# Decay and rate of an RWKV-7 mixer from three fp32r products each, in a hybrid decoder block

## Chip, cores and metric

One Trainium2 chip, one core of it. The metric is the device time of one execution in microseconds; the time before is 3533.41 us, the median of three runs (3525.39 to 3535.11).

## What is computed

One decoder block on 2048 tokens of width 1024, in float32. Half of the mixer's channels go through chunkwise retention, the other half through an RWKV-7 recurrence over 8 heads of 64 channels; then come a cross-attention into 256 memory tokens, a squared-ReLU MLP of width 4096 and a final norm. The change concerns two vectors of the recurrence, the decay and the rate `a`, which are made from low-rank factors (64 wide each):

```python
r, k, v, w_lr, a_lr, g_lr = jnp.split(p, [...], axis=-1)
w_log = -jax.nn.softplus(-(w0 + jnp.tanh(w_lr) @ w_up)) - 0.5
decay = jnp.exp(-jnp.exp(w_log))
a = jax.nn.sigmoid(a0 + a_lr @ a_up)
...
kk = kk / jnp.maximum(jnp.sqrt(jnp.sum(jnp.square(kk), axis=-1, keepdims=True)), 1e-12)
k = k * (1.0 + (a - 1.0) * k_a)
...
y = wkv7_scan(rh, decay.reshape(B, S, H, d), kh, vh, -kk, kk * ah)
```

## The kernel before

The kernel has two stages. The first (to about 1570 us in the profile) makes the projections, the retention, the recurrence and the products of the memory; the second (the output projection, the attention and the MLP) is not edited.

**Precision.** Large products take each operand as a sum of two fp32r parts, a rounded `hi` and a remainder `lo`, and add three products, hi·hi, hi·lo and lo·hi (`chain3_`). `split` (L181) makes the parts: ScalarE copies (L183), VectorE or GpSimd subtracts (L184). Small products are done in f32 with one call; the profile shows two records for such a call (two passes).

**Tiling of the first stage.** Four blocks of 512 tokens; in a block four pairs of heads, so 16 groups, numbered n = 4·block + pair. The names carry both: `mm13r` is the projection r of block 1, pair 3. The recurrence of a group runs over 8 chunks of 64 tokens.

**The functions around the change.** `lora_wa(b)` projects a block's 512 tokens on the two low-rank inputs, 128 rows in all (rows 0 to 63 of the decay, 64 to 127 of the rate): 24 fp32r products into `mmwa`, the token shift on ScalarE (L388) and VectorE (L389), then tanh on the rows of the decay (L794). The result `wa` has two buffers. `rwkv_prep(n, ...)` prepares a group. It loads the 128x128 factor `wua` (L405), makes the decay's argument `pz` from rows 0 to 63 and the rate's `pa` from rows 64 to 127 by one f32 product each, 128x512 in size, and takes tanh of both (`th` L410, `ta` L414). From `th` VectorE makes the running sums `cum` (L416, L419), ScalarE the exponentials; `sq`, its sums `pss`, the matrices `Mx` and the rest follow. `rwkv_chain` is the recurrence proper: three dependent products (`ch`) for each chunk, with small VectorE and ScalarE operations between them (`rh` L609, `X` L619, L620 and L630).

**What sets the order.** `weave` takes all of this as eight streams and records their instructions by a clock of its own, to which each product adds an assumed time (`mm`: N/2400 us for fp32r, four times that for a long f32 product). The TensorE order that results is kept as it is (`keep_in_program_order`); the other engines' queues are ordered by the scheduler's simulation. The stream `dense` issues the projections, taking for each block the first item of a list that is ready ("A" is `lora_wa`, "K" the keys, "R" the rest of a pair, "Q" the retention). `preps` starts a group once its keys and its block's `wa` are there.

Two pools matter: `ps_sc` has two PSUM buffers, used in turn, one each for `pz` and `pa`; `tp` has one SBUF buffer for a tag, so that all tiles with tag F use the same place one after the other: the retention's rotary part `rbq` (L719, read by GpSimd at L727), `b1` of the preparation, and others.

Of the kernel before, what the change touches and what calls it, by code (L numbers as in the profile page):

```python
# [8 lines left out]
F32 = mybir.dt.float32  # L9
F32R = mybir.dt.float32r  # L10
# [8 lines left out]
P = 128  # L19
# [17 lines left out]
BLK = 512  # L37
# [88 lines left out]
def hybrid_block(tc, a, out, dbg=None, halves=2, stages="012"):  # L126
    nc = tc.nc
    V, A, G, TE, SY, AQ = nc.vector, nc.scalar, nc.gpsimd, nc.tensor, nc.sync, nc.scalar
# [3 lines left out]
    def pinned(ins, us):  # L132

        if te["pin"]:
            tc.keep_in_program_order(ins)
            te["us"] += us

    def mm(o, l, r, start, stop):
        n = int(np.prod(r.shape[1:])) / 2400
        us = n if r.dtype != F32 else 4 * n if n > 0.05 else 0.03 if n < 0.02 else 0.084  # L140
        pinned(TE.matmul(o, l, r, start=start, stop=stop), us)  # L141
# [39 lines left out]
    def split(hi, lo, x, eng):  # L181

        A.activation(out=hi, in_=x, func=AF.Copy)  # L183
        eng.tensor_tensor(out=lo, in0=x, in1=hi.bitcast(F32), op=ALU.subtract)  # L184
# [96 lines left out]
    if "1" in stages:  # L281
        with ExitStack() as ctx:
            e = ctx.enter_context
            act = e(tc.tile_pool(name="act1", bufs=1))
            one = e(tc.tile_pool(name="one1", bufs=1))
            rp = e(tc.tile_pool(name="r1", bufs=1))
            tp = e(tc.tile_pool(name="t1", bufs=1))
            pp = e(tc.tile_pool(name="p1", bufs=1))
            gp = e(tc.tile_pool(name="g1", bufs=2))
            ps_mm = e(tc.tile_pool(name="mm1", bufs=2, space=PSUM))  # L290
            ps_sc = e(tc.tile_pool(name="sc1", bufs=2, space=PSUM))
# [90 lines left out]
            hs = [slice(0, 64), slice(64, 128)]  # L382
# [10 lines left out]
            def proj_cm(w, nm):  # L393
                ps = ps_mm.tile([P, BLK], F32, tag="mm", name=f"mm{nm}")
                yield from chain3_(ps, [((w[0][:, k, :], w[1][:, k, :]), (hT[0][:, :, k, :], hT[1][:, :, k, :])) for k in range(8)])
                return ps

            def rwkv_prep(n, pr, tok0, kS, wa, nm):
# [4 lines left out]
                g4 = [slice(0, 4), slice(4, 8)]  # L403
                lo_ = pp.tile([P, P], F32, tag="wua", name=f"wua{nm}", bufs=1)
                SY.dma_start(out=lo_, in_=a["lora"][pr][:, :P])  # L405

                pz = ps_sc.tile([P, BLK], F32, tag="sc", name=f"pz{nm}")
                mm(pz, lo_[0:64, :], wa[0:64, :], True, True)
                th = tp.tile([P, BLK], F32, tag="A", name=f"th{nm}")
                A.activation(out=th, in_=pz, func=AF.Tanh, scale=0.5, bias=w0h[:, pr : pr + 1])  # L410
                pa = ps_sc.tile([P, BLK], F32, tag="sc", name=f"pa{nm}")
                mm(pa, lo_[64:128, :], wa[64:128, :], True, True)
                ta = tp.tile([P, BLK], F32, tag="B", name=f"ta{nm}")
                A.activation(out=ta, in_=pa, func=AF.Tanh, scale=0.5, bias=a0h[:, pr : pr + 1])  # L414
                yield 0
# [50 lines left out]
                for q in range(8):  # L466
                    b = q % 4
# [319 lines left out]
                AQ.dma_start(out=yscr[tok0 // BLK][p * P : (p + 1) * P], in_=yo)  # L787

            def lora_wa(b):
                wa = one.tile([P, BLK], F32, tag="wa", name=f"wa{b}", bufs=2)  # L790
                w = W.load(a["w_rw"][12], (8, P), "w12")
                ps = yield from proj_cm(w, f"wa{b}")
                shifted(ps, 12, wa, f"wa{b}")
                A.activation(out=wa[0:64], in_=wa[0:64], func=AF.Tanh)  # L794
                return wa

            def lora_g(b):

# [39 lines left out]
            done = {("pg", -1): True, ("pg", -2): True, ("C", -1, 4): True, ("C", -1, NCH): True, ("C", -2, NCH): True, ("Y", -1): True, ("T", -1): True}  # L838
# [53 lines left out]
            def dense():  # L892

                for b in range(nb):
                    early = None
                    if b == 0:
                        early = yield from ret_proj(4, b, None, "v00")
                    yield lambda: ("X", b) in done
                    rt_ = rotary(b)
                    vs = {}  # L900

                    def ready(pr, what):
                        n = 4 * b + pr
                        if what == "A":
                            return n < 5 or ("P", n - 5) in done
                        if what == "K":
                            return ("P", n - 2) in done
                        if what == "R":
                            return ("P", n - 2) in done and (n < 4 or ("O", n - 4) in done)
                        if what == "Q" and pr == 3 and len(plan) > 1:  # L910
                            return False
                        if what == "Q":
                            return ("H", n - 2) in done
                        if what == "G":
                            return ("O", n - 1) in done
                        return True

                    plan = list(PLAN)
                    while plan:
                        yield lambda: any(ready(*i) for i in plan[:AHEAD])  # L920
                        item = next(i for i in plan if ready(*i))
                        plan.remove(item)
                        pr, what = item
                        n = 4 * b + pr
                        nm = f"{b}{pr}"
                        if what == "A":
                            done["wa", b] = yield from lora_wa(b)
                        elif what == "K":
                            done["K", n], = yield from rkv(b, pr, (1,))
                        elif what == "R":  # L930
                            done["R", n] = yield from rkv(b, pr, (0, 2))
                        elif what == "Q":
                            if pr % 2 == 0:
                                v, early = early, None
                                if v is None:
                                    v = yield from ret_proj(4 + pr // 2, b, rt_, f"v{nm}")
                                vs[pr] = vs[pr + 1] = v
                            sg = yield from ret_gate(b, pr)
                            qk = yield from ret_proj(pr, b, rt_, f"q{nm}", pr == 3)
                            done["Q", n] = qk, vs[pr], sg  # L940
                        elif what == "G":
                            done["G", b] = yield from lora_g(b)
                        elif what == "L" and b + 1 < nb:
                            xs.update({(b + 1, t): scaled_x(b + 1, t) for t in range(4)})
                        elif what == "L" and "0" in stages:
                            xs.update({("mem", t): scaled_memory(t) for t in range(2)})
                if "0" in stages:
                    W.alt, W.spare = True, (one, "gmix")
                    yield from memory()
                    W.spare = None  # L950
# [79 lines left out]
    if "2" in stages:  # L1030
        with ExitStack() as ctx:
# [4 lines left out]
            tp = e(tc.tile_pool(name="t2", bufs=2))  # L1036
# [376 lines left out]
```

## Time and profile before

| | |
|---|---|
| median of the runs | 3533.41 us |
| profiled execution | 3526.81 us, span 3525.0 us |
| TensorE busy | 3348.3 us, 95% of the span |
| VectorE, GpSimd, ScalarE busy | 2082.1, 1623.5, 1215.9 us |
| mean granted TensorE clock | 0.973 of 2.4 GHz |

Busy time counts a matmul from its start to its modelled end, and matmuls overlap; what one of them costs is read from the distance of starts in the timeline. A row of the timeline has the start, the duration, engine, line, operation, out<-in, the array rows and columns used where it is a matmul (64*128 is half of the rows), and in brackets the idle time ahead with its releaser.

### The profile page before, as it was taken

What the parts mean: (1) busy time and instruction counts of PE and PEld (TensorE: products, weight loads), DVE (VectorE), ACT (ScalarE), POOL (GpSimd) and SP (SyncE); (2) the same over time, 40 slices, a digit from 0 to 9 for tenths busy, and PEclk for the clock granted to TensorE, in tenths of its full rate; (3) what the DMA queues carried; (4) which work ended last, traced back from release to release, by engine and by line L of the source; (5) the groups of instructions that cost most, each with busy time, mean ns of one, the idle gap of its engine ahead of it and who ended that gap; (6) DMA issues with size and microseconds to landing.
All of it is one profiled execution on the core that took longest, in us unless ns stands there. A gap on an engine that the chain in (4) does not pass through costs nothing.

```text
span 3525.0 us, 57474 instructions
## 1 busy us (share of the span) xinstructions
PE 3348.3 (95%) x23296; PEld 2739.9 (78%) x23296; DVE 2082.1 (59%) x3637; ACT 1215.9 (34%) x1954; POOL 1623.5 (46%) x1325
## 2 busy tenths in 40 slices
PE   7889999999999899989999999999999999999998
PEld 6668777777777777878887888888788878888886
DVE  5765565456555644543866556555748665656557
ACT  4432323232323231334334333333433343333333
POOL 5444323232323232434546555555645465455555
PEclk9999999999999899999999999999999999999999
DMA  7434323332333233383111111111341111111111
GB/s 262 151 130 150 134 93 118 106 130 97 118 112 118 97 98 107 105 305 118 49 37 48 54 48 54 54 49 57 128 161 47 38 48 51 52 54 54 49 54 48
DMA packets 147160, 333.35 MB, mean 95 GB/s; under 512 B 52048, under 2 KB 62800, under 8 KB 146896
## 3 DMA queue, kind: packets, MB, share of 16 engines
q1 hardware_dynamic: 129632, 299.43, 25.5%
q10 hardware_dynamic: 17264, 30.26, 2.4%
q8 instruction: 183, 3.00, 0.3%
q14 instruction: 81, 0.66, 0.1%
HBM read 269.34 MB, written 60.29 MB: 94 GB/s over the span
## 4 chain that ended last, share of the span: by engine, by line
PE 49%; DVE 5%; POOL 2%; issue 1%; ACT 1%; DMA 0%; DVEq 0%; ACTq 0%; POOLq 0%
PE up L141 20%; PE o L141 4%; PE tms L141 4%; PE m3d L141 3%; PE m6d L141 3%; PE m1d L141 2%; PE m5d L141 2%; PE m4d L141 2%; PE m2d L141 2%; PE m7d L141 2%; DVE xr L1140 1%; DVE pe L1252 1%; PE pskv L141 1%; PE m3v L141 1%; PE psqk L141 1%
## 5 line engine op out<-in xcount | busy, mean ns | idle before, releaser
L141 PE MATMUL up<-uc,whi 128*128 128x512 f32 x2048 | 633.0, 390 | 4.8 <-ACT uc L1111 4.8
L141 PEld LDWEIGHTS up<-uc,whi 128*128 128x128 f32 x2048 | 384.6, 188 | 85.9 <-ACT uc L1111 5.7
L141 PE MATMUL up<-uc,wlo 128*128 128x512 f32 x1024 | 398.7, 390 | 0.0
L184 POOL TENSOR_TENSOR wlo<-wraw,whi 128x1024 fp32r<-128x1024 f32 x103 | 254.4, 2470 | 282.1 <-ACT whi L183 271.2
L183 ACT ACTIVATE whi<-wraw 128x1024 fp32r<-128x1024 f32 x175 | 184.8, 1058 | 398.7 <-PE up L141 139.7
L611 POOL TENSOR_SCALAR Sd<-X,PC 64x64 f32<-64x64 f32 x256 | 127.0, 496 | 351.5 <-DVE X L630 335.0
L184 DVE TENSOR_TENSOR wlo<-wraw,whi 128x1024 fp32r<-128x1024 f32 x72 | 104.6, 1454 | 256.5 <-ACT whi L183 256.4
L184 POOL TENSOR_TENSOR wlo<-s,whi 128x1024 fp32r<-128x1024 f32 x60 | 159.3, 2656 | 182.2 <-ACT whi L183 182.2
L141 PEld LDWEIGHTS up<-uc,wlo 128*128 128x128 f32 x1024 | 192.3, 188 | 40.1
L141 PE MATMUL tms<-whi,ub 128*128 128x256 f32 x1024 | 192.2, 286 | 0.0
L184 POOL TENSOR_TENSOR wlo<-bd,whi 128x1024 fp32r<-128x1024 f32 x64 | 165.9, 2594 | 52.3 <-ACT whi L183 52.2
L184 POOL TENSOR_TENSOR f<-au,f 128x1024 fp32r<-128x1024 f32 x40 | 112.1, 2801 | 133.6 <-ACT f L183 133.6
L141 PE MATMUL o<-whi,f 128*128 128x512 f32 x512 | 162.8, 398 | 1.5 <-issue 1.5
L141 PEld LDWEIGHTS tms<-whi,ub 128*128 128x128 f32 x1024 | 161.1, 191 | 0.4
L141 PE MATMUL rmq<-whi,hh 128*128 128x256 f32 x512 | 151.6, 296 | 0.0
L141 PE MATMUL rmq<-whi,hl 128*128 128x256 f32 x512 | 151.2, 295 | 0.0
L141 PE MATMUL rmq<-wlo,hh 128*128 128x256 f32 x512 | 150.9, 295 | 0.0
L1299 ACT ACTIVATE au<-up 128x512 f32<-128x512 f32 x128 | 75.1, 587 | 204.9 <-PE up L141 204.9
L141 PE MATMUL tms<-wlo,ub 128*128 128x256 f32 x512 | 145.4, 284 | 0.0
L619 ACT ACTIVATE X<-ch,rn 64x64 f32<-64x64 f32 x128 | 39.1, 306 | 303.6 <-PE Y L141 269.7
L1071 POOL TENSOR_TENSOR s<-bd,bd 128x1024 f32<-128x1024 f32 x48 | 122.2, 2548 | 30.1 <-DMA bd<-w_down 21.8
L183 ACT ACTIVATE whi<-bd 128x1024 fp32r<-128x1024 f32 x64 | 67.7, 1057 | 189.3 <-PE m2d L141 63.6
(1061 smaller groups left out, 9177.8 us busy)
## 6 DMA issues: line engine op xcount, KB each, us to landing
bd<-w_down SPq DMA_DIRECT2D x64, 512.0 KB
wraw<-w_up SPq DMA_DIRECT2D x64, 512.0 KB
whi<-kepthiw SPq DMA_DIRECT2D x45, 512.0 KB
wlo<-keptlow SPq DMA_DIRECT2D x45, 512.0 KB
whi<-kepthim SPq DMA_DIRECT2D x36, 512.0 KB
wlo<-keptlom SPq DMA_DIRECT2D x36, 512.0 KB
wraw<-w_out SPq DMA_DIRECT2D x32, 512.0 KB
xs<-x SPq DMA_DIRECT2D x16, 512.0 KB
```

The lines of the kernel that those rows point to most:

```text
L141: pinned(TE.matmul(o, l, r, start=start, stop=stop), us)
L183: A.activation(out=hi, in_=x, func=AF.Copy)
L184: eng.tensor_tensor(out=lo, in0=x, in1=hi.bitcast(F32), op=ALU.subtract)
L611: G.tensor_scalar(out=Sd[hs[h], :], in0=X[h][g][hs[h], i, :], scalar1=PC[hs[h], c : c + 1], scalar2=None, op0=ALU.mult)
L619: A.activation(out=X[0][g][hs[0], i, :], in_=chp[hs[0], 64:128], func=AF.Copy, scale=rn[hs[0], c : c + 1])
L1071: eng.tensor_tensor(out=into, in0=x, in1=y, op=op)
L1140: V.tensor_tensor(out=xv, in0=xv, in1=ps, op=op)
L1252: V.tensor_scalar(out=pe[:, t, :], in0=pe[:, t, :], scalar1=sm[:, t : t + 1], scalar2=None, op0=ALU.mult)
L1299: A.activation(out=r, in_=ps, func=AF.Relu)
```

## The change

The factor and `wa` are both split into two fp32r parts, and each of the two products becomes three, interleaved: `pz` and `pa` in turn. `wa` goes first into the shared buffer F (as `wf`), then into two parts with one buffer each; for that the "A" step of a block now waits until the last group ahead of it has issued these products, where it waited for the end of a group's preparation five groups back.

```diff
                 lo_ = pp.tile([P, P], F32, tag="wua", name=f"wua{nm}", bufs=1)
                 SY.dma_start(out=lo_, in_=a["lora"][pr][:, :P])
+                wu = [pp.tile([P, P], F32R, tag=f"wu{i}", name=f"wu{i}{nm}", bufs=1) for i in range(2)]
+                split(*wu, lo_, V)
 
                 pz = ps_sc.tile([P, BLK], F32, tag="sc", name=f"pz{nm}")
-                mm(pz, lo_[0:64, :], wa[0:64, :], True, True)
+                pa = ps_sc.tile([P, BLK], F32, tag="sc", name=f"pa{nm}")
+                for i, (l, r) in enumerate(((0, 0), (0, 1), (1, 0))):
+                    for h, ps in enumerate((pz, pa)):
+                        mm(ps, wu[l][hs[h], :], wa[r][hs[h], :], i == 0, i == 2)
+                done["z", n] = True
                 th = tp.tile([P, BLK], F32, tag="A", name=f"th{nm}")
                 A.activation(out=th, in_=pz, func=AF.Tanh, scale=0.5, bias=w0h[:, pr : pr + 1])
-                pa = ps_sc.tile([P, BLK], F32, tag="sc", name=f"pa{nm}")
-                mm(pa, lo_[64:128, :], wa[64:128, :], True, True)
                 ta = tp.tile([P, BLK], F32, tag="B", name=f"ta{nm}")
...
             def lora_wa(b):
-                wa = one.tile([P, BLK], F32, tag="wa", name=f"wa{b}", bufs=2)
+                wa = tp.tile([P, BLK], F32, tag="F", name=f"wf{b}")
...
                 A.activation(out=wa[0:64], in_=wa[0:64], func=AF.Tanh)
-                return wa
+                parts = [one.tile([P, BLK], F32R, tag=f"wa{i}", name=f"wa{i}{b}", bufs=1) for i in range(2)]
+                split(*parts, wa, V)
+                return parts
...
                         if what == "A":
-                            return n < 5 or ("P", n - 5) in done
+                            return n < 4 or ("z", n - 1) in done
```

First place: TensorE's order at the fourth group of block 1 (`TT` and `TC` belong to the inversion of `Mx`, `Y` is the recurrence's output). Before:

```order
L141 MATMUL mm13r<-hl,whi_6254 128x512
L141 MATMUL ch_2_6342<-rh_2_6344,TT_162 64x64 x2
L141 MATMUL Y_6173<-AR_11_0_5089,X_11_0_5366 64x64
L141 MATMUL Y_6173<-AR_11_0_5092,X_11_0_5368 64x64
L141 MATMUL pz_6396<-wa_4047,wua_6394 128x512
L141 MATMUL pa_6400<-wa_4047,wua_6394 128x512
L141 MATMUL ph_2_6404<-TT_161,TC_6328 16x16 x32
L141 MATMUL ch_2_6342<-X_11_0_5366,BKt_0_5386 64x64
```

The same place in the change (`wu_13` and `wa` appear as two tiles each, hi with the lower number):

```order
L141 MATMUL mm13r<-hl,whi_6318 128x512
L141 MATMUL ch_2_6406<-rh_2_6408,TT_162 64x64 x2
L141 MATMUL Y_6237<-AR_11_0_5141,X_11_0_5422 64x64
L141 MATMUL Y_6237<-AR_11_0_5144,X_11_0_5424 64x64
L141 MATMUL pz_6464<-wa_4146,wu_13_6460 128x512
L141 MATMUL pa_6465<-wa_4146,wu_13_6460 128x512
L141 MATMUL pz_6464<-wa_4147,wu_13_6460 128x512
L141 MATMUL pa_6465<-wa_4147,wu_13_6460 128x512
L141 MATMUL pz_6464<-wa_4146,wu_13_6461 128x512
L141 MATMUL pa_6465<-wa_4146,wu_13_6461 128x512
L141 MATMUL ph_2_6476<-TT_161,TC_6392 16x16 x32
L141 MATMUL ch_2_6406<-X_11_0_5422,BKt_0_5442 64x64
```

Six products stand where two stood; the neighbours are the same.

Second place: ScalarE's queue at the third group of block 2 (`ts22k` and `kk` belong to this group's keys, `Pe` and `Pi` are its exponentials). Before:

```order
L388 ACTIVATE ts22k<-mm22k,pv 128x512
L430 ACTIVATE kk_9501<-kS22k,pv 128x512
L410 ACTIVATE th_9466<-pz_9464,dv 128x512
L414 ACTIVATE ta_9470<-pa_9468,dv 128x512
L750 ACTIVATE qkTR_9523<-pqR_9518 128x512
L423 ACTIVATE Pe_9494<-cum_9485 128x8x64
```

In the change:

```order
L388 ACTIVATE ts22k<-mm22k,pv 128x512
L434 ACTIVATE kk_9589<-kS22k,pv 128x512
L183 ACTIVATE wu_23_10348<-wua_10346 128x128
L416 ACTIVATE th_9568<-pz_9560,dv 128x512
L418 ACTIVATE ta_9570<-pa_9561,dv 128x512
L754 ACTIVATE qkTR_9623<-pqR_9618 128x512
L427 ACTIVATE Pe_9582<-cum_9573 128x8x64
```

The copy of the next group's factor (`wu_23`) has come in ahead of this group's `th`; it is so in all groups but the last of the stage, and the difference on VectorE stands at the like place.

Third place: VectorE's queue at the start of block 1, around the token shift of `mmwa` (`RsR` belongs to the retention). Before:

```order
L620 TENSOR_SCALAR X_03_0_3401<-ch_0_4058,rn_2730 64x64
L630 SCALAR_TENSOR_TENSOR X_03_0_3399<-ch_0_4058,PC_2618,Sd_0_4059 64x64
L630 SCALAR_TENSOR_TENSOR X_03_0_3401<-ch_0_4058,PC_2618,Sd_0_4059 64x64
L389 SCALAR_TENSOR_TENSOR wa_4047<-mmwa_4052,dv,tswa_4110 128x512
L609 COPY rh_1_4127<-ch_1_4125 128x64
L741 SCALAR_TENSOR_TENSOR RsR_4139<-prR_4134,cs 128x512
```

In the change:

```order
L624 TENSOR_SCALAR X_03_0_3475<-ch_0_4105,rn_2778 64x64
L389 SCALAR_TENSOR_TENSOR wf_4074<-mmwa_4079,dv,tswa_4140 128x512
L634 SCALAR_TENSOR_TENSOR X_03_0_3473<-ch_0_4105,PC_2656,Sd_0_4106 64x64
L634 SCALAR_TENSOR_TENSOR X_03_0_3475<-ch_0_4105,PC_2656,Sd_0_4106 64x64
L745 SCALAR_TENSOR_TENSOR RsR_4174<-prR_4169,cs 128x512
L184 TENSOR_TENSOR wa_4147<-wf_4074,wa_4146 128x512
L613 COPY rh_1_4186<-ch_1_4184 128x64
```

The shift has moved ahead of the two X of the chain, and the new difference stands between them and the chain's `rh`.

## Rows read from the trace of the kernel before

**Rows 1.** Page: busy time, share of the span and instructions of each engine.

```profile
PE 3348.3 (95%) x23296; PEld 2739.9 (78%) x23296; DVE 2082.1 (59%) x3637; ACT 1215.9 (34%) x1954; POOL 1623.5 (46%) x1325
```

**Rows 2.** Windows: length, busy us (instructions) by engine, PE clock, DMA share, GB/s.

```profile
core 0: us, PE busy (x) PEld busy (x) DVE busy (x) ACT busy (x) POOL busy (x), PEclk, DMA share, GB/s
0.00:1290.00 1290.00, 1183.79 (x11855) 936.15 (x11855) 741.67 (x1842) 405.61 (x798) 459.31 (x729) 0.95 0.39 129
```

**Rows 3.** TensorE's waits, 0 to 1330 us: total us, times, longest us.

```profile
PE ch L141 <- DVE X L620: 24.0, 17, 5.4
PE pk L148 <- ACT X L512: 13.0, 5, 5.9
...
PE pss L141 <- ACT sq L432: 0.6, 1, 0.6
```

**Rows 4.** Page: chain that ended last, share of the span by engine.

```profile
PE 49%; DVE 5%; POOL 2%; issue 1%; ACT 1%; DMA 0%; DVEq 0%; ACTq 0%; POOLq 0%
```

**Rows 5.** Timeline of TensorE at the first group.

```profile
53.54 0.39 PE L141 MATMUL mm00r<-hh,whi 128*128 128x512 f32 x1
53.86 0.69 PE L141 MATMUL pz<-wa,wua 64*128 64x512 f32 x1
53.87 0.69 PE L141 MATMUL pa<-wa,wua 64*128 64x512 f32 x1
54.39 0.59 PE L141 MATMUL pz<-wa,wua 64*128 64x512 f32 x1
54.40 0.59 PE L141 MATMUL pa<-wa,wua 64*128 64x512 f32 x1
54.92 0.50 PE L141 MATMUL mm00r<-hl,whi 128*128 128x512 f32 x1
```

**Rows 6.** Tile `pz`: duration in ns, min/median/max, first and last start in us.

```profile
L141 PE MATMUL pz<-wa,wua x32: 589/641/693, 53.9 to 1290.9; 64*128 64x512 f32 x32
```

**Rows 7.** Timeline of TensorE at a full-height f32 product of 512 columns.

```profile
1286.44 0.39 PE L141 MATMUL mm33r<-hh,whi 128*128 128x512 f32 x1
1286.68 1.02 PE L141 MATMUL pb<-rS32r,cs 128*128 128x512 f32 x2
1287.62 0.34 PE L141 MATMUL ch<-X,AR 128*64 128x64 f32 x4
```

**Rows 8.** Timeline of TensorE, f32 products of 128 columns, full and half height.

```profile
374.74 1.05 PE L141 MATMUL prR<-rv,rq 128*128 128x128 f32 x8
375.63 0.60 PE L148 MATMUL pqR<-cs,rq 128*128 128x128 f32 x4
...
381.39 1.26 PE L141 MATMUL rsR<-qkTR 64*128 64x128 f32 x16
382.59 0.34 PE L141 MATMUL ch<-X,AR 128*64 128x64 f32 x4
```

**Rows 9.** Timeline of TensorE behind the pair of block 1, fourth group.

```profile
574.81 1.08 PE L141 MATMUL ph<-TT,TC 32*16 32x16 f32 x64 [0.82 <-issue]
```

**Rows 10.** Tiles `lw` and `hl`: duration in ns, min/median/max, first and last start.

```profile
L668 ACT ACTIVATE lw<-gup x16: 298/310/312, 15.4 to 1443.2; 96x128 fp32r<-96x128 f32 x16
L669 DVE TENSOR_TENSOR lw<-gup,lw x16: 283/283/1271, 21.9 to 1443.9; 32x128 fp32r<-32x128 f32 x16
L321 DVE TENSOR_TENSOR hl<-psta,hh x32: 678/691/692, 14.3 to 1073.1; 128x512 fp32r<-128x512 f32 x32
```

**Rows 11.** VectorE's wait for `th`, 0 to 1330 us.

```profile
DVE th L416 <- ACT th L410: 26.4, 14, 2.9
```

**Rows 12.** Timelines: TensorE and ScalarE in block 0; GpSimd, VectorE, TensorE in block 1.

```profile
46.06 0.39 PE L141 MATMUL mm00k<-hh,whi 128*128 128x512 f32 x1
48.26 0.63 ACT L794 ACTIVATE wa<-wa 64x512 f32<-64x512 f32 x1
...
363.42 1.42 POOL L727 TENSOR_TENSOR rq<-rq,rbq 128x256 f32<-128x256 f32 x2 [2.54 <-DVE rbq L724]
...
374.70 0.22 DVE L609 COPY rh<-ch 128x64 f32<-128x64 f32 x1
...
376.62 0.33 PE L141 MATMUL ch<-rh,TT 64*64 64x64 f32 x4
```

## Prediction

> **What bounds the kernel now.** The page first: TensorE is busy 95% of the span and the next engine, VectorE, 59% [rows 1]. The change touches only the first part of the kernel, so I asked for the stretches of that part. From 0 to 1290 us TensorE is busy for 1183.8 us; only 106 us are without a matmul in flight, and its granted clock is 0.95 on average, so nearly all of it at the upper of its two levels, 2.4 GHz [rows 2]. Who TensorE waits for comes next: the recurrent chain's X (24.0 us in 17 waits), then copies of `pvt` (13.0 in 5); the head of the preparation, which this change edits, shows up once with 0.6 us, as `pss` waiting for `sq` [rows 3]. So a microsecond less on TensorE in this part is a microsecond less in the end, unless one of these waits follows directly and takes it up. After this part the chain that ended last is almost wholly TensorE work and weight splits [rows 4]; nothing there is edited, and the later stage only starts earlier or later.
>
> **What the two products cost now.** The timeline of TensorE around the first group shows four records: first pass of `pz` at 53.86 and of `pa` at 53.87, second passes at 54.39 and 54.40, next projection at 54.92 [rows 5]. Both products lie on top of each other (one in rows 0 to 63 of the array, the other in 64 to 127), in two passes of 0.53 us: 1.06 us for the pair. All 16 groups read alike (32 records each, 589 to 693 ns, in the view of the tile) [rows 6]. So the old code never paid for two f32 products one after the other; 16 x 1.06 = 17.0 us is all there is to win.
>
> **What the six products will cost.** A 512-column fp32r product comes 0.23 to 0.24 us after the one ahead of it in the stream of projections (1286.44 to 1286.68, one of many such steps) [rows 7]. Three of them after one another take 0.69 us if the `pz` and `pa` product of each step overlap fully, and six take 1.38 us if they don't overlap at all. No row shows an fp32r pair on half arrays, so the f32 rows decide. A full-height f32 pass of 512 columns takes (1287.62 - 1286.68)/2 = 0.47 us with the gap behind it, 0.42 to 0.43 without [rows 7]; the same pass in the pair takes 0.53, a factor of about 1.24. At 128 columns, eight full-height passes take 375.63 - 374.74 = 0.89 us, 0.11 each, and 16 records on half arrays, so eight pair passes, 382.59 - 381.39 = 1.20, less a gap of 0.09 as below, 0.14 each: 1.25 [rows 8]. Two widths, one factor, so I take 0.23 x 1.25 = 0.28 us a step and 0.85 us a group: 0.21 us less than 1.06. The ends are 0.37 less (full overlap) and 0.32 more (none).
>
> The gaps around the pair I leave in: 53.54 to 53.86 is 0.32, 0.09 more than a step [rows 5], and I take the same behind it. The f32 product `pb`, which uses the full height, follows an fp32r product after 0.24, without a gap [rows 7], so it is the half array and not the number format that costs it, and the six new products are still on half arrays. The Trainium skill, "TensorEngine Tiling (Array Packing)", Tiling Modes, says that changing the tiling mode drains the engine; by that rule, with which the rows agree, the gaps stay. Were they the format's, another 0.2 us a group would go, and a group would win up to 0.57: the cheap end of the range.
>
> **Which groups keep it.** In the fourth group of blocks 1, 2 and 3 the pair is followed by `ph`, which waits 0.82 us for the copy TC [rows 9]; a faster pair lengthens that wait. In the change's order this neighbour remains in blocks 1 and 3 (the first place shown with the change) and has gone in block 2. 14 groups keep their gain: 14 x 0.21 = **-2.9 us** (ends: 16 x -0.57 = -9.1, 16 x +0.32 = +5.1).
>
> **What is added beside it.** Per group a copy of 128x128 on ScalarE and a difference on VectorE: about 0.31 and 0.28 us by the like operations on `lw` [rows 10]. Both stand directly ahead of `th`, and what they split is the next group's factor (second place). ScalarE: `th` comes 0.31 later behind the copy, but the pair ends 0.21 earlier: 0.10 us. VectorE waits there anyway, 26.4 us in 14 groups, for `th` [rows 11]; the difference falls into that wait. `th` leads to `sq`, for which TensorE waited 0.6 us in all [rows 3]: **0**, and 16 x 0.10 = 1.6 if that cover were gone. The factor's transfer now waits for the split of the group before and not for its products, so it is issued about a group ahead of its use (82 us on average: 16 groups from 53.9 to 1290.9 [rows 6]): 0. In block 0 it has moved up in SP's queue and waits there for the first split, with the load of the key weights behind it; TensorE needs those at 46.06 [rows 12], some 20 us later: 0. At the start the first split adds one VectorE operation ahead of an `hl` for which TensorE waits: **+0.3** (0 to 0.6).
>
> Per block, ScalarE copies 128x512 (0.63 by the tanh of `wa` [rows 12]) and VectorE subtracts 128x512 (0.69 by `hl` [rows 10]). In block 1 the difference stands ahead of `rh`, the recurrent chain's next operation, and waits for tanh and copy (third place): up to 0.7 in each of three blocks, 2.1 in all. In the trace the chain's consumer of that `rh` comes at 376.62, 1.7 us after `rh` was ready (374.70 + 0.22), with other products ahead of it [rows 12], so most is covered: **+0.4**. For block 0, `wa` is ready at 48.26 + 0.63 = 48.89 and needed at 53.86 [rows 5, 12]; copy and difference, 1.3 us, fit in. The new condition on the "A" step costs nothing: the projections come in the same sequence, with `mmwa` ahead of the next block's first key projection as before.
>
> Sum: -2.9 + 0.3 + 0.4 = **-2.2 us**. The profiled execution took 3526.8 us (span 3525.0), so 3524.6; the median of the runs lies 6.6 us above it, and I forecast that median: 3533.4 - 2.2 = **3531 us**, no change that can be told: what a measurement can tell here is about 0.3%, 10.6 us.
>
> **Rivals.**
> *Full overlap.* A step takes 0.23, a group 0.69: 14 x -0.37 + 0.7 = -4.5, 3529 us, and down to 3533.4 - 9.1 + 0.7 = 3525 if the gaps went too. For it: both records of a pair start 0.01 us apart. Against it: 0.53 for a pass of 0.43. The Trainium skill, "TensorE: Matmul & The Clock Gate", Part 3, Measured speedup vs the span model, has packed row tiles take one product's duration plus some 4 ns a tile; as an estimate by that page a group is 0.70 us, the time of this rival, and the rows of the f32 pair don't bear it out.
> *No overlap (slower).* If fp32r products on half arrays come one after the other, a group takes 1.38: 16 x 0.32 = +5.1, + 0.7 = +5.8, 3539 us. It decides from 0.35 us a step (1.06/3) on. For it: no fp32r pair has been seen. Against it: nothing in the f32 pairs hints at a difference by format.
> *The order moves.* Positions on all engines shift a little in this part, since the recording sums its own times for products. The stalls are single events: up to 5.9 us for one `pk`, 5.4 for one X [rows 3]. Two of that size more or less make about 10 us either way: 3521 to 3541. Against it: the sequence of projections is the same, and only single chain steps changed place.
> *F's slot.* `wf` now lives in the one buffer F, whose last reader before it is GpSimd's `rq`: done at 363.42 + 1.42 = 364.84 in block 1, while the write comes just ahead of the `rh` at 374.70, some 9 us later [rows 12]. Later than that, VectorE would stop with the chain's operations behind it, one us for each us late, three times: it would need 4 us in each block to be seen.
>
> **How the numbers follow.** Forecast as summed 0.50 (3531), full overlap 0.22 (3529 to 3525), no overlap 0.10 (3539), order moved 0.15 (half each way), F's slot 0.03. The range of 3518 to 3541 takes in the cheap end (3525) with one long stall fewer (-5.9, so 3519), and no overlap with a little more; some of the moved orders are left out. Faster by over 0.3% needs the cheap end with luck in the order, or a moved order alone: 0.06 + 0.10 = 0.16. Slower by over 0.3% needs no overlap and 5 us more, or a moved order: 0.09. The rest, 0.75, is no change that can be told.
>
> **What would show it.** In the changed profile: six records for `pz` and `pa` a group, in three steps of about 0.28 us (0.23 full overlap, 0.46 none), and 0.85 us from `pz` to what follows; the gaps of 0.10 on both sides; `th` within 0.1 us of where it was behind the pair; VectorE's wait for `th` smaller; TensorE's idle time from 0 to 1290 within some us of 106; the last stage as long as before. The prediction is wrong if a group takes over 1.06 us, if a wait by `pz` for a split appears, or if the waits of rows 3 change by 10 us.

## The result and the profile after

The changed kernel takes **3502.8 us** (median of 4 runs, 3498.7 to 3505.4), the kernel before, over the 4 runs beside it, 3532.4: a ratio of 0.992, interval 0.9904 to 0.9937. It is 29.5 us faster, where no change that can be told was forecast, and 15 us below the low end of the range. The profiled execution took 3505.4 us (span 3503.4).

The products themselves did nearly what the forecast said. The timeline of TensorE at the first group of the changed kernel (the place of [rows 5]):

```profile
56.70 0.39 PE L141 MATMUL mm00r<-hh,whi 128*128 128x512 f32 x1
57.02 0.50 PE L141 MATMUL pz<-wa,wu 64*128 64x512 f32 x1
57.02 0.50 PE L141 MATMUL pa<-wa,wu 64*128 64x512 f32 x1
57.36 0.39 PE L141 MATMUL pz<-wa,wu 64*128 64x512 f32 x1
57.37 0.39 PE L141 MATMUL pa<-wa,wu 64*128 64x512 f32 x1
57.59 0.39 PE L141 MATMUL pz<-wa,wu 64*128 64x512 f32 x1
57.60 0.39 PE L141 MATMUL pa<-wa,wu 64*128 64x512 f32 x1
57.92 0.50 PE L141 MATMUL mm00r<-hl,whi 128*128 128x512 f32 x1
```

The two halves of a step start together, a step takes 0.23 us (57.36 to 57.59) with 0.11 more behind the first step and 0.10 behind the last (57.59 to 57.92), and a group 0.90 us where it took 1.06. Over 16 groups that is 2.6 us, a tenth of the gain (in this profile one group, at 245.96 us, ran at half the clock and took 1.58). The first group also starts 3.2 us later than before (57.02 against 53.86). The tile's rows cover all 16 groups, with the time at which the last one came, 20.3 us sooner than in [rows 6]; VectorE's wait for `th` has all but gone [rows 11]:

```profile
L141 PE MATMUL pz<-wa,wu x48: 385/395/792, 57.0 to 1270.6; 64*128 64x512 f32 x48
```

```profile
DVE th L420 <- ACT th L416: 3.0, 8, 0.9
```

So the time was gained between the groups. TensorE's waits from 0 to 1330 us (columns as in [rows 3]) have other sizes: X fell from 24.0 to 13.4 us, its longest from 5.4 to 2.8, and `pg`'s wait for TA (a part of the inversion of `Mx`) grew from 7.2 to 15.9. Before:

```profile
PE pg L141 <- DVE TA L589: 7.2, 8, 1.6
```

and after:

```profile
PE pg L141 <- DVE TA L593: 15.9, 9, 4.6
PE ch L141 <- DVE X L624: 13.4, 16, 2.8
PE pk L148 <- ACT X L516: 12.7, 7, 3.8
...
PE pss L141 <- ACT sq L436: 1.2, 1, 1.2
```

So the two largest changes nearly cancel (31.2 us for X and TA before, 29.3 after). Which single wait shrinks doesn't make the gain either: `e3` below, as fast as the changed kernel, waits 21.4 us for X and 3.9 for TA.

Where stage 1 ends (the first `o` product) makes the account. Windows of the kernel before up to there and behind it (columns as in [rows 2]):

```profile
0.00:1572.20 1572.20, 1442.87 (x14177) 1155.85 (x14177) 886.19 (x2165) 495.40 (x955) 561.57 (x836) 0.95 0.40 133
```

```profile
1572.20:3525.00 1952.80, 1905.45 (x9120) 1584.07 (x9120) 1195.91 (x1472) 720.49 (x999) 1061.89 (x489) 0.99 0.19 63
```

and of the changed kernel, with the stretch behind it:

```profile
0.00:1551.00 1551.00, 1432.17 (x14209) 1150.15 (x14209) 890.92 (x2185) 502.30 (x975) 557.73 (x836) 0.96 0.40 135
```

```profile
1551.00:3503.00 1952.00, 1904.78 (x9120) 1584.51 (x9120) 1195.95 (x1472) 720.95 (x999) 1061.46 (x489) 0.99 0.19 64
```

Stage 1 is 21.2 us shorter, the rest as long as before (1952.8 and, to the end of its span of 3503.4, 1952.4). TensorE stood without a matmul for 129.3 us before and for 118.8 now: 10.5 us of stalls have gone, 4.0 of them a single one on instructions ("Instruction blocks" below). Half-speed time makes the other half: one minus the granted clock, summed over slices of 4 us, comes to 78.6 us before and 68.3 after, 10.3 less (some 7 us of either pass within stalls and are counted twice). What is left after both is the same, 1364.3 and 1363.9 us. Most stretches at a granted clock of 0.50 (1.2 GHz) begin during or shortly behind one of the longer stalls (1.3 to 5.9 us): up to 1330 us 18 of 19 in the profile before, 14 of 20 in the changed one; the others don't.

One place shows how stall and clock hang together: group 11. The kernel before, timeline of TensorE (idle time in brackets):

```profile
860.55 0.69 PE L141 MATMUL ph<-TT,TC 32*16 32x16 f32 x64 [1.11 <-ACT TC L578]
863.85 0.48 PE L141 MATMUL ch<-X,BKt 128*64 128x64 f32 x4 [2.61 <-DVE X L620]
864.26 0.48 PE L141 MATMUL Y<-SR,X 64*64 64x64 f32 x4
864.67 2.08 PE L141 MATMUL rsR<-qkTR 64*128 64x128 f32 x16
```

and the changed kernel:

```profile
858.73 0.72 PE L141 MATMUL ph<-TD,Mx 32*32 32x16 f32 x64 [0.86 <-DVE TD L579]
859.38 1.16 PE L141 MATMUL rsR<-qkTR 64*128 64x128 f32 x16
861.16 0.34 PE L141 MATMUL ch<-X,BKt 128*64 128x64 f32 x4 [0.62 <-DVE X L624]
861.42 0.33 PE L141 MATMUL Y<-SR,X 64*64 64x64 f32 x4
861.69 0.69 PE L141 MATMUL ph<-TT,TC 32*16 32x16 f32 x64
```

The written order has moved `rsR` ahead of the chain's step and `ph` behind it. The time that the chain needs for X now passes in part under `rsR`: waits of 1.11 and 2.61 us have given way to 0.86 (for TD) and 0.62. The windows behind that place, of before and then of after:

```profile
861.20:872.00 10.80, 7.46 (x98) 6.05 (x94) 8.11 (x17) 2.49 (x8) 4.62 (x6) 0.60 0.01 2
872.00:882.00 10.00, 10.00 (x121) 8.40 (x121) 1.98 (x6) 2.22 (x5) 1.15 (x3) 0.74 0.01 2
```

```profile
861.20:872.00 10.80, 9.69 (x211) 7.79 (x211) 6.90 (x16) 3.60 (x9) 4.27 (x5) 0.84 0.01 2
872.00:882.00 10.00, 10.00 (x101) 7.63 (x94) 4.10 (x11) 2.38 (x5) 4.26 (x9) 1.00 0.34 90
```

Before, the granted clock was 0.60 and 0.74 on the mean of these windows, 21 us behind the stall; after, 0.84 and 1.00: 6.9 us of full speed lost against 1.7. From this group to the next it took 73.3 us before and 64.0 after. How much of that is `rsR`'s is not shown, for other rows of the stretch moved with it: `e2` below, with the same written order, still waits 2.04 us for X behind `rsR` and takes 71.4, and `e1`, with the old order, waits only 0.55 for X, but 4.63 and 1.77 for TA just behind, and takes 75.1.

### The profile page after: what moved, and what is told of

It reads as the page before. It is cut to its first block, busy times and chain, and to the rows that moved or that the text cites. A ratio compares the mean times of both kernels' runs of the same rounds, so it can differ in the third digit from the quotient of the medians.

```text
span 3503.4 us, 57596 instructions
## 1 busy us (share of the span) xinstructions
PE 3337.0 (95%) x23328; PEld 2734.7 (78%) x23328; DVE 2086.9 (60%) x3657; ACT 1223.3 (35%) x1974; POOL 1619.2 (46%) x1325
## 4 chain that ended last, share of the span: by engine, by line
PE 50%; DVE 5%; issue 2%; ACT 1%; POOL 1%; DVEq 0%; POOLq 0%; ACTq 0%
PE up L141 20%; PE o L141 4%; PE tms L141 4%; PE m3d L141 3%; PE m6d L141 3%; PE m4d L141 2%; PE m2d L141 2%; PE m1d L141 2%; PE m5d L141 2%; PE m7d L141 2%; DVE xr L1146 2%; DVE pe L1258 1%; PE pskv L141 1%; PE m3v L141 1%; PE psqk L141 1%
## 5 line engine op out<-in xcount | busy, mean ns | idle before, releaser
L141 PE MATMUL rmq<-whi,hh 128*128 128x256 f32 x512 | 150.5, 294 | 0.0
```

## The experiments

**Theory 1**: the gain comes from the moved order. The list maker (`weave`, with `mm`'s sum of times) counts 1.28 us for six fp32r products where it counted 1.71 for two f32 ones, so single steps of the chains land elsewhere; stalls and the half clock behind them differ. **Theory 2**: it comes from the cheaper products and what they release. **Theory 3**: from `lora_wa`'s split and tag F. A fifth, on instruction blocks, came up later; there was no fourth. The other new condition, on the step "A", was not run apart; `e1` keeps it, and its order on TensorE is that of the kernel before but for some six rows. Ratios are to the kernel before in the same job.

### Order and arithmetic apart

`e1` is the changed kernel with the old count, `e2` the kernel before with the new one:

```diff
 # e1, behind the six products
+if te["pin"]:
+    te["us"] += 2 * 4 * 512 / 2400 - 6 * 512 / 2400
 # e2, behind the two f32 products
+if te["pin"]:
+    te["us"] -= 2 * 4 * 512 / 2400 - 6 * 512 / 2400
```

> The changed kernel, whose list maker now counts the six products at 1.71 us a group, the count that the two f32 products had, instead of 1.28. The written order of TensorE then stands as in the kernel before, but for 6 rows of some 13,580 (the change moved some 520); the six fp32r products, the splits and tag F are all kept. Theory 1 (the gain of 29.5 us comes from the moved order, by shorter stalls and fewer stretches at half the clock): the gain goes, 3527 to 3535 us; what is left of it is the products' own time, 16 x 0.16 = 2.6 us, less some 3 us that the start lost. Theory 2 (the gain comes from the cheaper products and what they release earlier): the gain stays, 3499 to 3506 us. Theory 3 (it comes from lora_wa's split and tag F, which change ScalarE's and VectorE's queues): it stays too, 3499 to 3506 us. The waits would show it: by theory 1 pk<-ACT X of 5.9 us and ch<-X of 5.4 us are back, by the others they stay gone.

> The kernel before, its two f32 products kept, with only the list maker's count for them set to 1.28 us a group instead of 1.71. TensorE's written order is then row for row that of the changed kernel (the products themselves aside); no split, no tag F. Theory 1: the gain is had without the change's arithmetic, 3500 to 3508 us (the f32 pair costs 16 x 0.16 = 2.6 us more, the start some 3 us less than in the changed kernel). Theories 2 and 3: no gain, 3528 to 3536 us.

`e1`: 3524.4 us, ratio 0.9994 [0.9978, 1.0010]. With the old order all the gain has gone, the products notwithstanding: theories 2 and 3 fall as the sole cause. But the waits that theory 1 named did not come back as they were: the longest for X is 4.7 us, the longest of `pk` for X 3.1, and TA has 24.6 in all. `e2`: 3519.7, ratio 0.9976 [0.9958, 0.9993], about a third of the gain and by its interval at most about half, between what either theory allowed, so theory 1 alone falls too. Its profile has the stalls of the new order (1570.7 us to the end of stage 1, of it 118.2 without a matmul) but more time at half clock, 85.3 us.

### The products' own time

`e3` issues three products of `pz`, then three of `pa`; `e4` only high x high.

```diff
 # e3
-for i, (l, r) in enumerate(((0, 0), (0, 1), (1, 0))):
-    for h, ps in enumerate((pz, pa)):
+for h, ps in enumerate((pz, pa)):
+    for i, (l, r) in enumerate(((0, 0), (0, 1), (1, 0))):
 # e4
+for h, ps in enumerate((pz, pa)):
+    mm(ps, wu[0][hs[h], :], wa[0][hs[h], :], True, True)
+if te["pin"]:
+    te["us"] += 4 * 512 / 2400
```

> The changed kernel with the three products of pz first and then the three of pa, instead of by turns; TensorE's written order is otherwise the same. A group took 0.90 us from its first product to the next work where a half of rows 0 to 63 and a half of rows 64 to 127 followed each other (0.34, 0.23, 0.33 us a pair). If that overlap comes from the turns, six products in a row of at least 0.21 us each take 1.28 us or more, and 16 groups lose at least 16 x 0.38 = 6 us. Theory 1 and theory 2: 3503 + 6 to 8 = 3509 to 3511 us if the loss stands on the path to the end, no stall being shortened by it; 3503 where the two products of equal half overlap as well or the loss falls into stalls.

> The changed kernel with the high x high product alone (the two products with a low part are left out, so decay and rate are rougher), the list maker's count held at 1.28 us a group, so that TensorE's written order stands but for some 7 rows. A group should take about 0.34 us instead of 0.90: 16 x 0.56 = 9 us less of TensorE. Theory 2 (the products' time is what counts, and more than their own length is gained from each microsecond): 3494 us or less, by the ratio of the change itself (29.5 us for 2.6 us of products) far less. Theory 1: 3494 us at best, where every microsecond of TensorE reaches the end, and up to 3503 where stalls take it up.

`e3`: 3500.7 us, 0.9918 [0.9892, 0.9943], no loss. Its timeline shows why: the halves overlap as before, though issued three and three:

```profile
55.42 0.50 PE L141 MATMUL pz<-wa,wu 64*128 64x512 f32 x1
55.43 0.50 PE L141 MATMUL pa<-wa,wu 64*128 64x512 f32 x1
55.76 0.39 PE L141 MATMUL pz<-wa,wu 64*128 64x512 f32 x1
55.77 0.39 PE L141 MATMUL pa<-wa,wu 64*128 64x512 f32 x1
```

`e4`: 3511.1, 0.9951 [0.9933, 0.9969], some 10 us slower than the changed kernel and outside what either theory allowed (3503 at most), although a group takes 0.43 us instead of 0.90 (56.37 to 56.80). Up to the end of stage 1 (1558.0 us) the time that is neither stall nor half clock is 1356.4, 7.5 less than in the changed kernel, which is 16 x 0.47. Stalls have 124.7 us (5.9 more) and half clock 76.9 (8.6 more). A microsecond less on TensorE did not come out at the end. Its groups also show what surrounds a step: one step of 0.23 us takes 0.43, so 0.20 is added behind it.

### Other orders

The count set to 0.85 and to 2.13 us, for either arithmetic; some 585 and 795 of 13,580 rows of TensorE then stand elsewhere than before. The changed kernel again beside them.

```diff
 if te["pin"]:
-    te["us"] += 2 * 4 * 512 / 2400 - 6 * 512 / 2400
+    te["us"] += 0.85 - 6 * 512 / 2400        # or 2.13; with the f32 pair less 2 * 4 * 512 / 2400
```

> The changed kernel itself, once more, beside the three that follow. 3499 to 3506 us by every theory; with 12 runs it shows how far its runs scatter, and whether their granted clock stays at 0.976 to 0.978 where that of the kernel before was 0.973 on the mean of 28 runs.

> The kernel before, f32 products kept, with the list maker's count for a group's two products set to 0.85 us (1.71 in the kernel before). Some 585 of TensorE's 13,580 rows then stand elsewhere than before, and some 740 elsewhere than in the changed kernel: a third order. Theory 1, as it stands after the first four runs (each written order has its own stalls, 110 to 130 us of them up to the end of stage 1, and the half-clock stretches that follow them; the products' time is a few us): 3505 to 3540 us, with no rule from the count to the time. Theory 2 (the order matters only as far as the cheaper products let it): 3520 to 3532, as the other two with f32 products (3525.9 and 3519.7).

> The kernel before with that count at 2.13 us a group: some 795 rows of TensorE moved against the kernel before, a fourth order. Theory 1: 3505 to 3540 us, another figure than at 0.85, 1.28 and 1.71 by some us. Theory 2: 3520 to 3532 us.

> The changed kernel with that count at 2.13 us a group: the same order on TensorE as the run before this one, but for 5 rows. Theory 1: within 10 us of that run, since the order is the same and the products' own time is some 3 us. Theory 2: 15 us or more under it, since the cheaper products gain whatever the order.

> The changed kernel with the list maker's count at 0.85 us a group: the order of the run with the f32 pair at that count (3522.6 us), but for one row on TensorE. Theory 1 with 5: 5 to 14 us under that run, 3508 to 3518 us, for the stall near 1170 us is gone and the products cost some 3 us less. Theory 2: 3500 to 3505 us. No wait of over 2 us put down to issue, by theory 5.

Ratio to the kernel before:

| count, us a group | f32 pair | six fp32r products |
|---|---|---|
| 0.85 | 0.9990 [0.9975, 1.0005] | 0.9947 [0.9928, 0.9966] |
| 1.28 (the change's) | 0.9976 [0.9958, 0.9993] | 0.9920 [0.9904, 0.9937], again 0.9931 [0.9906, 0.9956] |
| 1.71 (the old one) | 1 | 0.9994 [0.9978, 1.0010] |
| 2.13 | 0.9995 [0.9977, 1.0012] | 0.9962 [0.9948, 0.9977] |

Each row of the table has one written order on TensorE, but for some ten rows. Both theories miss half: with the f32 pair the order makes 0 to 0.24%, and the fp32r products, with all that goes with them, bring nothing at the old order and 0.33 to 0.56% at the three others, four to eight times their 2.6 us (0.07%). `r4` came 12.6 us under `r3`, where theory 1 said within 10 and theory 2 at least 15; `r5` (3512.8 us) lies where theory 1 together with theory 5 below put it. The change's order has the lowest ratio in either column, though its intervals overlap with those at 0.85, and the sizes don't follow the count.

### Instruction blocks

The four kernels with the f32 pair run so far all had one stall near 1170 us put down to "issue" in their profiles (3.4 to 4.0 us), the six with fp32r products none (rows of the kernel before):

```profile
1166.57 0.64 PE L141 MATMUL ph<-TT,TC 32*16 32x16 f32 x58
1171.19 0.24 PE L141 MATMUL ph<-TT,TC 32*16 32x16 f32 x6 [3.99 <-issue]
```

It comes here in the middle of one series of equal products, and in all four behind 10,746 to 10,753 matmul records (the expectation of `t1` has other counts), and the DMA view of 1166 to 1171.2 us has one packet of instructions (183 of them are 3.00 MB over the span, so 16 KB) among 0.98 MB of other traffic:

```profile
q1 hardware_dynamic: 839, 0.98, 53.2%
q8 instruction: 1, 0.02, 1.2%
```

**Theory 5**: TensorE's instructions arrive in blocks, and one comes late where it meets bulk loads; six products in place of two shift the blocks. Dummy products whose result is overwritten shift them alone, first of 128x1 (`t`), then of 32x32 (`u`, `v`):

```diff
 ps = ps_sc.tile([P, 4, P], F32, tag="sc", name=f"psta{b}{t}{g}")
+if (b, t, g) == (0, 0, 0):
+    for _ in range(14):          # 14, 50 or 64
+        ins = TE.matmul(ps[0:32, 0, 0:32], ident[0:32, 0:32], ident[0:32, 0:32], start=True, stop=True)
+        if te["pin"]:
+            tc.keep_in_program_order(ins)
```

> The kernel before with 14 f32 products of 128x1 (two passes each, so 28 pairs of a weight load and a matmul) ahead of the first transposes, where TensorE stands idle for 11 us; their result is overwritten. Theory 5 (the four kernels with the f32 pair all show one stall of 3.4 to 4.0 us put down to issue near 1170 us, always behind some 11,182 to 11,189 matmul records, while a 16 KB instruction packet lands within it; the six with the fp32r products, which have issued 28 more pairs there, show none: TensorE's instructions come in blocks, and one block comes late where it meets the bulk loads of whi and wlo and the Lscr stores): the shift takes the stall away, and with it its half-clock stretch (8.6 us lost at 1168 to 1188 in the profile before): 3514 to 3522 us, no wait of over 2 us put down to issue. Theories 1 and 2: 3524 to 3528 us as the kernel before, since order and arithmetic are kept (TensorE's order but for some 10 rows).

> The changed kernel with 50 such products there: 100 pairs, which with the 28 pairs of the change make 128, the number that lies between two instruction packets in the profile before (125 to 144 pairs in the slices from 1115 to 1153 us), so that the blocks begin near group 13 where they did in the kernel before. Theory 5: a stall of 3 to 4 us put down to issue comes back near 1150 us, with a half-clock stretch behind it: 3504 to 3512 us. Theories 1 and 2: 3499 to 3504 us.

> The kernel with the f32 pair and the changed kernel's written order (3519.7 us), with the 14 dummy products of the first of these four. Theory 5 together with theory 1 (order and the place of the instruction blocks together make the gain): 3506 to 3513 us, most of the way to the changed kernel's 3499 to 3503, and no long wait put down to issue. Theory 2: 3517 to 3522 us.

`t1`: 3526.3 us, 0.9980 [0.9964, 0.9997]; `t2`: 3520.1, 0.9973 [0.9960, 0.9987]; `t3`: 3507.2, 0.9941 [0.9918, 0.9965]. The stall left `t1` and `t3` and came back in `t2` (2.31 us), as theory 5 has it; `t3` met its number, `t1` missed it, and `t2` was slower than any theory said. But `t2`'s dummies took 0.21 us each and started the program 15 us late, and `t1`'s moved ten rows. So the test was made again without these two faults (in `u2` and `u4` some rows of the other engines still moved, in `u1` and `u3` none):

> The kernel before with 14 f32 products of 32x32 (28 pairs) ahead of the first transposes, in TensorE's idle time; every engine's order is as before. Theory 5 (instruction blocks): the stall of 4 us near 1170 us is gone, the stretch from the 14th group's products to the 15th's falls from 68.5 us to 56 to 60; of the time 4 to 10 us go: 3516 to 3523 us beside 3526 for the kernel before, ratio 0.997 to 0.9985. Theory 1 alone (order): no change, 3524 to 3529, ratio 0.999 to 1.001.

> The kernel before with 64 such products (128 pairs, the number between two instruction packets): the blocks begin where they did. Theory 5: the stall near 1170 us stays, ratio 0.999 to 1.001. If the dummies as such took it away, it is gone here too and the ratio is that of the run before this one.

> The changed kernel with 50 such products (100 pairs; with the change's own 28 near group 13 a full block); every engine's order is the changed kernel's. Theory 5: a stall of 2 to 4 us put down to issue near 1150 us, the stretch from the 14th group's products to the 15th's at 63 to 68 us instead of 58 to 60, and 4 to 10 us on the time: 3504 to 3512 us, ratio 0.994 to 0.9965 to the kernel before. Theory 1 alone: 3498 to 3503 us, ratio 0.992 to 0.9935.

> The changed kernel with 64 such products (128 pairs): the blocks where the changed kernel has them. Theories 1 and 5: no stall near 1150 us, 3498 to 3504 us, ratio 0.992 to 0.9935 (VectorE's order differs by some 18 of 3270 rows).

The stall goes and comes as theory 5 says. In `u1` it is gone; in `u2`, a full block, it is back ahead of the same six records:

```profile
1169.93 0.64 PE L141 MATMUL ph<-TT,TC 32*16 32x16 f32 x58
1174.86 0.24 PE L141 MATMUL ph<-TT,TC 32*16 32x16 f32 x6 [4.30 <-issue]
```

In `u3` one of 1.62 us appears at 1151.42, in `u4` none. The times do not follow: `u1` 3525.9 (1.0002 [0.9987, 1.0016]) and `u2` 3526.8 (0.9996 [0.9984, 1.0008]), `u3` 3502.5 (0.9929 [0.9917, 0.9941]) and `u4` 3505.2 (0.9937 [0.9924, 0.9950], 1 us above its range). So the stall is real, and in the profiles its stretch is 7 us longer (group 14 to 15, 57.5 in `u1` and 64.5 in `u2`), but at the old order with the f32 pair, and at the new one with the fp32r products, it makes no difference between the medians: theory 5 falls as the cause of the gain. Whether it counts with the f32 pair at the new order is the question of `v1`. Why the block comes late is not shown; that bulk loads are in its way was not varied.

### The last two

`v1` repeats `t3` with the small dummies; `v2` is the changed kernel whose splits are made, but whose products are the f32 pair on the unsplit tiles (`mm(ps, lo_[hs[h], :], wa[2][hs[h], :], True, True)`, `wf` in a buffer of its own).

> The f32 pair with the changed kernel's written order and 28 pairs of 32x32 dummies ahead of the first transposes; all engines' orders are those of the kernel with the f32 pair and the new order (ratio 0.9976, interval 0.9958 to 0.9993). If the place of the instruction blocks counts once the order is the new one: ratio 0.9925 to 0.9955, as the earlier try (0.9941). If the earlier try was a draw: 0.996 to 0.999.

> The changed kernel with its splits of wu and wa and its list maker's count, but the products done as the f32 pair from the unsplit tiles (the shifted tile wf in a buffer of its own); TensorE's order is the changed kernel's, the other engines' that of the f32 pair with the new order but for the splits themselves. If the splits and the queues they lengthen give the gain: ratio 0.992 to 0.9945. If the fp32r products and what they shift give it: 0.9955 to 0.999, as with the f32 pair and the new order (0.9976).

`v1`: 3512.9, 0.9954 [0.9940, 0.9969], between `e2` and `t3` and at the upper end of the range that it was given if the blocks count. All engines' orders are those of `e2`. `v2`: 3515.4, 0.9972 [0.9954, 0.9990], as `e2`: the splits give nothing (tag F is not in `v2`; it is in `e1`, which gained nothing), theory 3 falls. The four kernels with the f32 pair and the change's order lie at 0.9976, 0.9941, 0.9954 and 0.9972, on the mean 0.996: **14 us, about half of the gain, come without the change's products.** The pairs differ, though. `e2` and `v2`, which have the stall on instructions, gain 9 us on the mean, and that is the order alone; `t3` and `v1`, whose shifted blocks have lost the stall, gain 18.5. The intervals of `e2` and `v1` overlap, so whether the place of the blocks adds to the new order there is open.

Where it does so stands in the profiles. Time from the first product of a group to that of the next, us (differences of starts in the timelines; groups counted from 1):

| stretch | old order: before, u1, u2, e1 | new order, f32 pair: e2, t3, v1, v2 | new order, fp32r: after, r1, e3, u3, u4 |
|---|---|---|---|
| group 4 to 5 | 156.0, 155.9, 155.9, 155.1 | 150.3, 149.0, 147.9, 150.5 | 146.9, 150.6, 147.1, 145.3, 146.7 |
| group 8 to 9 | 172.5, 176.9, 172.9, 170.7 | 179.3, 175.9, 175.7, 179.5 | 172.7, 166.7, 172.5, 173.4, 176.9 |
| group 11 to 12 | 73.3, 73.3, 73.2, 75.1 | 71.4, 65.0, 66.1, 67.1 | 64.0, 64.0, 66.4, 64.0, 64.0 |
| group 14 to 15 | 68.5, 57.5, 64.5, 56.9 | 63.9, 58.8, 60.2, 65.0 | 59.5, 58.2, 57.9, 62.0, 58.2 |

Two stretches fall with the order, whatever the arithmetic: group 4 to 5 by 6.3 (f32) and 8.4 us (fp32r) on the means, group 11 to 12 by 6.3 and 9.2; `e1`, with fp32r products, has neither. Group 14 to 15 is long where the instruction stall is (before, `u2`, `e2`, `v2`, shorter in `u3`). In group 8 to 9 the new order with the f32 pair loses 4.3 us on the means against the old one; with the fp32r products it does not.

## Why the prediction was wrong, and where it was right

**The step that failed** is the rival "The order moves": "Two of that size more or less make about 10 us either way", with half of 0.15 on this side; in the sum of -2.2 us the moved order stands at nothing. The runs showed that the gain hangs on it: with the order put back and the products kept (`e1`) the ratio is 0.9994, and with the order alone (`e2`, `v2`) 9 us are gained. The mechanism was named (the recording sums its own times for products); its size was taken from the stalls' lengths alone, and the sign left to chance because "the sequence of projections is the same, and only single chain steps changed place". The stretch from group 11 to 12, where `rsR` and `ph` change place about a chain's step, is alone 6 to 9 us shorter on the means. The order could be read before the run, and the trace held the stall of 2.61 us at that place; whether weighing the moved rows against the stalls one by one would have given the size was not tried. One sign of being wrong that the prediction named did come, the wait for X changed by 10.6 us.

**The price of a stall** left out the clock. [Rows 2] were read as a clock that is nearly always at its upper level. But 10.3 of the 20.8 us that stage 1 lost in stalls and half clock were half clock, most of it behind stalls. By these two profiles "about 10 us" for two stalls of 5 us should have been about 20; by the whole of stage 1 before (78.6 us of half clock on 129.3 of stalls) about 16. The ratio is not fixed: `e2` has fewer stalls than the kernel before and more half clock (118.2 and 85.3).

**TensorE as the bound.** "A microsecond less on TensorE in this part is a microsecond less in the end, unless one of these waits follows directly" is refuted by `e4`: 7.5 us less work, 14.5 us more in stalls and half clock.

**The six products.** The step is 0.23 us, not 0.28. What was read as a factor of 1.24 on a 512-column pass fits better as 0.20 us added to a group, 0.10 behind its first step and 0.10 behind its last, while the gap ahead of the group stayed (56.70 to 57.02, 0.32 as in [rows 5]). Three fp32r steps are then 3 x 0.23 + 0.20 = 0.89 us (measured 0.90), one step in `e4` 0.43 (0.43), and two f32 passes, each 0.43 as the prediction read a full-height one, 1.06 (1.06). By that estimate the old pair overlapped fully too, and the rows of 512 columns don't speak against the full-overlap rival; at 128 columns [rows 8] it doesn't fit (0.89 + 0.20 = 1.09, measured 1.20). The group took 0.90 (forecast 0.85), the saving 2.6 us (2.9). The two groups set aside because `ph` would wait longer behind a faster pair kept theirs: the wait was 0.82 us before and is 0.82 and 0.73 now. By the rule that the full-overlap rival named (the Trainium skill, "TensorE: Matmul & The Clock Gate", Part 3, Measured speedup vs the span model) packed row tiles cost one product's duration plus some 4 ns for each further tile; the trace agrees with it for a step in fp32r, 0.23 against 0.23 for one full-height product; the 0.20 of the group come on top.

**The start** was forecast 0.3 us later and is 3.2 later at the first group in the profile (2.6 and 1.6 in `r1` and `e3`, and in `u4` 0.2 earlier). It had gone by group 5 (392.83 against 392.38). The splits cost nothing that can be told (`v2`), the wait for `th` shrank, the condition on "A" moved nothing on TensorE (`e1`), the write into F's slot waited for `tswa` and for no reader of F, and the last stage kept its length: these stood.

**What stays open.** The order with the f32 pair gives 9 us, with the blocks shifted 18.5. The changed kernel's order with fp32r products gives 26 on the mean of five measurements (0.9920, 0.9931, 0.9918, 0.9929, 0.9937), so the products and what comes with them bring 7 to 17 us more there, 0.3 to 0.4% at two other orders and nothing at the old one, and only some 3 are their own time. Over the 123 runs of the kernel before that stand beside the experiments, the mean granted clock is 0.9726, over the 10 of the changed one 0.9774; within a kernel, runs differ by about 28 us of span for 0.01 of clock, so 13 us go with the clock. Why the clock stays higher there than in most kernels with the f32 pair (0.9732, 0.9770, 0.9753 and 0.9747 in `e2`, `t3`, `v1` and `v2`) was not found. The other queues are not the same for the two arithmetics (about 50 of VectorE's 3270 rows stand elsewhere), and no run holds them fixed, so they remain an untested rival for this part.

No experiment beat the changed kernel: `e3`, 3500.7, lies within its runs.

## What to carry to other kernels

Where a generator orders the instructions by times that it counts itself, an edit of one operation's cost is an edit of the order everywhere behind it: compare the two written orders at each of the long stalls before pricing the operation. Price a stall with the half-clock stretch that follows it in the trace; in stage 1 here the half clock cost about 0.6 us for each microsecond of stall. To tell order from arithmetic, keep the one and change the other, by the count alone; that costs two kernels and showed here that neither makes the gain alone, which comparing two profiles could not.

## What the runs showed of the hardware

TensorE's instructions come in blocks of 16 KB, here 183 for 23,296 pairs of weight load and matmul (about 127 each), and a block can come late: 3.4 to 4.3 us of idle time at one count of instructions in the kernels with the f32 pair, removed by 28 pairs ahead (`u1`), back after 128 (`u2`). Data transfers took 53% of the DMA engines' time just then; that they are the reason is not shown.

Two fp32r products on the two halves of the array's rows overlap fully (0.23 us a step for both), whether written by turns or three and three (`e3`). With 512 columns a group takes about 0.20 us more than its steps: 0.90 us for three, 0.43 for one (`e4`).

Runs of one kernel scatter by up to 29 us (3515.8 to 3545.1, the kernel before in one job) with the granted clock, so a profile is one draw: that of `u1` was 10 us under its mean span (3515.1 against 3525.0).
